# Five of the seven additions of squares in three norms, sent as accumulating transfers on GpSimd's queue

## Chip, cores and metric

One NeuronCore of a Trainium2 chip runs the whole program. The metric is the device time of one execution in microseconds; before, the median of 3 runs is 1616.66 us (1616.23 to 1616.78).

## The reference, cut to what matters

A trunk of two layers is applied to two groups of tokens, 512 and 256, which the kernel handles as 768 columns (`T`). The model has 1024 features, eight blocks of 128 rows.

```python
def rms_norm(x, g):
    y = xf * lax.rsqrt(jnp.mean(xf * xf, axis=-1, keepdims=True) + EPS)
    return y * g
...
for i in range(DEPTH):
    h = rms_norm(x, norm_mix[i])
    x = x + (window_attention(h, ...) if i % 2 == 0 else short_conv(h, ...))
    h = rms_norm(x, norm_mlp[i])
    x = x + jnp.square(jax.nn.relu(h @ mlp_w_up[i])) @ mlp_w_down[i]
    gate = jax.nn.sigmoid(rms_norm(x, norm_ple[i]) @ ple_w_gate[i])
    x = x + (p[i] @ ple_w_proj[i]) * gate
return rms_norm(x, final_norm)
```

## The kernel before, in words

**Precision and products.** Every factor is split into a high and a low half (`hi` by ScalarE, `lo` as a subtraction on VectorE), and each product takes three matmuls. Wide products use a scheme with seven instead of eight block products (`Norm7`, `Weights7`, `seven_parts`, line 2013), for which weights and activations are also summed and split (`q`, `t`, `sum`, `zhi`, `whi`, `vhi` and their low halves). The order inside one `seven_parts` is: product w11 into bank a, copy c of a (line 2030), product s3 into b, copy p, product s2 into a, copy d of a (line 2042), and so on. TensorE can't write on in bank a before ScalarE has made c, and again d.

**A norm.** The input of a norm comes in eight blocks, in the order 0, 4, 1, 5, 2, 6, 3, 7 (`PAIRED`, line 1911). For each block `Norm7.block` (line 729) splits the scaled block and calls `square` (line 620): the first block's square is written to `acc` by ScalarE (line 623); each later one goes to a temporary `sq` on ScalarE (line 626) and is added to `acc` by VectorE (line 627), seven additions of 128x768. When all are in, `acc` is split into `ah` and `al` (line 498 and 499), TensorE sums over the partitions by a matmul with ones (`ss`, line 666), and logarithm, exponential and one Newton step give the factor that later results are multiplied by. The products behind the norm start before the factor is known.

**The three norms of the change** are n1 (before the first MLP, its blocks come from the attention's output product), n3 (before the convolution, blocks from the gated layer `ple`) and n4 (before the second MLP, blocks from the convolution's output product). I call them norm 1, 3 and 4. Norm 2 and 5 (class `Norm`) keep their additions on VectorE.

**GpSimd's queue.** It issues accumulating transfers for two other purposes: `gathered` (line 830 to 837) sums pieces of the first weights behind norm 1 and norm 3 (four each), and `shared` (line 2224 to 2232) adds `p` to two halves of `x` in the MLPs (96 in all, 192 KB each). Its memory for descriptors is 512 bytes per partition (line 54).

**Buffers.** `sq`, `q`, `ah`, `al` and other temporaries share a ring of six buffers (`big`, line 580): a buffer can be written again when its last reader is done.

**The order of the work.** Behind the attention stage every operation is recorded, with a cost and a lag from `Recorder.add` (line 233), and `Recorder.end` (line 284) fixes the order of every engine from these estimates; then everything is issued in that order. A transfer on GpSimd's queue is entered with cost 3.5 and lag 5.0. Each engine runs its list in order, and waits on semaphores where a datum comes from another engine or from a transfer. GpSimd waits likewise: a transfer into `acc` is issued when the one before has landed.

Of the kernel before, what the change touches and what calls it, by code (L numbers as in the profile page):

```python
# [14 lines left out]
F32 = mybir.dt.float32  # L15
# [3 lines left out]
ALU = mybir.AluOpType  # L19
# [4 lines left out]
P = 128  # L24
# [3 lines left out]
T = sum(SEQS)  # L28
# [22 lines left out]
ROWS = 32  # L51
EXP_LN = "natural_log_exp_and_others"

BACC = dict(dynamic_dma_scratch_size=512)


class Tile:
# [89 lines left out]
class Recorder:  # L147
# [85 lines left out]
    def add(self, engine, what, run, outs, ins, line, table=None):  # L233
        n = max([1] + [size(ap) for ap in outs])
        if engine == "PE":
            cost = {384: 0.1735, 256: 0.121, 512: 0.23, 128: 0.11}.get(n, n * 0.45e-3)
            lag = cost + 0.16
        elif engine == "DVE":
            cost = 0.07 + n * 1.042e-3 + 0.06 * (what == "scalar_tensor_tensor" and n > 384)
            lag = cost + 0.082  # L240
        elif engine == "ACT" and what == "dma_start":
            cost, lag = 0.1, 4.0
        elif engine == "ACT":
            cost = 0.032 + n * 0.911e-3 + 0.09 * (len(ins) > 1)
            lag = cost + 0.095
            if table is not None:
                if table != self.tables[0]:
                    cost += 1.3
                    lag += 1.3
        elif engine == "SP":  # L250
            cost, lag = 0.46, 4 * P * n / 350e3
        elif what == "dma_start":
            cost, lag = 3.5, 5.0
        else:
            cost, lag = 0.3, 0.4
        op = Recorded(engine, run, cost, lag, line)
        op.size, op.due = n, self.due
        for ap in ins:
            self.touch(op, ap, False)
        for ap in outs:  # L260
            self.touch(op, ap, True)
        if self.also is not None:
            op.pre[self.also] = True
        if table is not None:
            if self.tables[1] is not None:
                op.pre.setdefault(self.tables[1], False)
            self.tables = table, op
        self.ops.append(op)
        return op
# [187 lines left out]
def trunk_kernel(ctx: ExitStack, tc: tile.TileContext, a: dict, out: bass.AP):  # L457
    nc = tc.nc
# [6 lines left out]
    const = ctx.enter_context(tc.tile_pool(name="const", bufs=1))  # L465
# [16 lines left out]
    sink = const.tile([P, HEADS], F32, name="sink")  # L482
    nsink = const.tile([P, HEADS], F32, name="nsink")
    ident = const.tile([P, P], F32, name="ident")
    make_identity(nc, ident[:])
    sparks = const.tile([P, P], BF16, name="sparks")
    dve.memset(sparks[:], 1.0)
    ones32 = const.tile([P, P], F32, name="ones32")
    dve.memset(ones32[:], 1.0)
    ones = const.tile([P, P], F32R, name="ones")  # L490
    dve.tensor_copy(ones[:], ones32[:])
    eps = const.tile([P, 1], F32, name="eps")
    dve.memset(eps[:], EPS)

# [104 lines left out]
    class Norm:  # L599


        n = T

        def __init__(self, i, name, places, acc, rstd=None):
            self.i, self.name, self.places, self.rplace = i, name, places, rstd
# [14 lines left out]
        def square(self, m, xb):  # L620
            if not self.begun:
                self.begun, self.acc = True, slot(self.aplace, f"acc_{self.name}", F32)[:, : self.n]
                act.activation(self.acc, xb, AF.Square)
            else:
                sq = self.temp("sq")
                act.activation(sq, xb, AF.Square)
                dve.tensor_tensor(self.acc, self.acc, sq, ALU.add)

        def temp(self, name, dt=F32):
            if more is not None:  # L630
# [16 lines left out]
                    act.preload_act_table_set(EXP_LN)  # L647
            self.ready = True

        def sum_squares(self, psum, also=None, parts=None, tag=None):  # L650

            n = self.n
            ah, al = parts or self.acc_parts()
            terms = [(ones, ah), (ones, al)]
            if also is not None:
                sq = self.temp("sq")
                dve.tensor_tensor(sq, also, also, ALU.mult)
                terms.append((ones32, sq))
            if more is None:
                t = psum.tile([P, 1024], F32, tag="mm", name="ss")  # L660
                out = [(t[:, :512], 0, 512), (t[:, 512:n], 512, n)]
            else:
                out = pieces(both("ss", tag)) if n == T else [(fresh("ss")[:, :n], 0, n)]
            for t, o, e in out:
                for i, (w, z) in enumerate(terms):
                    pe.matmul(t, lhsT=w[:], rhs=z[:, o:e], start=i == 0, stop=i == len(terms) - 1)
            return out
# [2034 lines left out]
    def conv_sources(n):  # L2702

        m = 2 * (n // 3) + (KB, 2 * KB, 0)[n % 3]
        return a["w_in"][m], a["w_in"][m + 1]
# [136 lines left out]
    held0 = [xs0[i] for i in (1, 2, 4, 5, 7, 8, 10, 11, 26, 27)] + act0[:2] + xs0[12:16] + act0[2:3]  # L2842

    n1 = Norm7(2, "mlp0", xs0[:12], act0[11], apart=xs0[12:], aside=act0[1])
    behind, product, w0 = second_inputs(n1, act0[7:11])
    w = [weight(a["w_o0"][2], 4)] * 2
    w2 = weight(a["w_o2"], 2, tag="z")
# [24 lines left out]
    act1 = ls[:7] + hs[4:8] + free[24:26] + ls[7:]  # L2872

    n3 = Norm7(1, "mix1", xs2, act0[9], aside=xs0[10])
    w2, behind = first_chunk(conv_sources(0), n3, 2, True)
    ple(n2, n3, act0[10:13], behind, w)

    n4 = Norm7(3, "mlp1", xs1, act1[11])
    w1, behind = first_chunk((a["up"][1, 0], a["up"][1, 2]), n4, 3, False)
    mixer_conv(n3, *w2, 2, n4, wide, xs0[16], ys, hs, ls, behind, (act0[13], xs0[11]))  # L2880
    spare = [xs1[i] for i in (21, 10, 11, 17, 0, 7, 14, 12, 13, 18, 19, 20, 24, 25)]
# [89 lines left out]
```

## Time and profile before

| | |
|---|---|
| median of 3 runs | 1616.66 us |
| the profiled execution: its time, its span | 1616.74 us, 1614.9 us |
| granted clock of TensorE | 0.998 |
| busy TensorE, VectorE, ScalarE, GpSimd | 1604.0, 1385.1, 958.9, 107.0 us |
| blocks of norm 1, norm 3, norm 4 | about 259 to 282, 774 to 828, 1010 to 1067 us |
| one addition of squares on VectorE | 0.945 us |

In rows of a timeline the columns are: start and duration in us, engine, line of the kernel, operation, written tile and read tiles, shape, count, and in brackets the idle time before and what ended it. In a list of waits they are: total us, times, longest. The busy time of TensorE contains the overlap of matmuls that follow each other, so a lost tenth of a microsecond shows rather in the distance of their starts. "issue" as a releaser means that the profile shows nothing that was waited for.

### The profile page before, as it was taken

To read this page: it belongs to the slowest core of one execution; us is meant where nothing else is said; L and a number is where in the kernel's file an instruction comes from. 1 tells how busy PE (TensorE), PEld (TensorE's weight loads), DVE (VectorE), ACT (ScalarE), POOL (GpSimd) and SP (SyncE) were. 2 spreads that over 40 slices of the span, in tenths; PEclk is the share of its full clock that TensorE was granted. 3 is DMA by queue.
4 is the path that set the end of the run, shared out by engine and by line. 5 is a ranking of instruction groups with operands and counts; after the bars stand their busy time and mean duration, and the time that the engine had idled before them with its cause. 6 is when DMAs were issued, how large, how long until landed. Compare 5 with 4: busy or idle time off the path is not lost.

```text
span 1614.9 us, 24411 instructions
## 1 busy us (share of the span) xinstructions
PE 1604.0 (99%) x9259; PEld 1556.6 (96%) x9259; DVE 1385.1 (86%) x2255; ACT 958.9 (59%) x1529; POOL 107.0 (7%) x166
## 2 busy tenths in 40 slices
PE   9999999999999999999999999999999999999997
PEld 7988889999999999999999999999999999999987
DVE  7579997998888888999899777789888888889985
ACT  7378887765555555556674434565555555556655
POOL 1001000010110110100000000000110111010000
PEclk9999999999999999999999999999999999999999
DMA  8745314233443343315312211112343343342232
GB/s 299 212 122 151 110 37 131 105 112 85 117 108 92 100 104 93 106 66 154 105 61 93 73 69 68 66 66 88 97 104 92 103 117 85 86 118 79 87 119 88
DMA packets 63953, 168.42 MB, mean 104 GB/s; under 512 B 7867, under 2 KB 23611, under 8 KB 63836
## 3 DMA queue, kind: packets, MB, share of 16 engines
q1 hardware_dynamic: 48716, 145.24, 26.8%
q0 software_dynamic: 14976, 21.50, 8.1%
q8 instruction: 72, 1.18, 0.3%
q14 instruction: 45, 0.37, 0.1%
q10 hardware_dynamic: 144, 0.13, 0.0%
HBM read 128.05 MB, written 9.96 MB: 85 GB/s over the span
## 4 chain that ended last, share of the span: by engine, by line
PE 95%; ACT 2%; DVE 2%; issue 1%; DMA 0%; SPq 0%; DVEq 0%; ACTq 0%
PE a L943 39%; PE b L943 10%; PE mm L435 8%; PE d L943 6%; PE c L943 5%; PE mm L557 5%; PE gate L557 4%; PE B L943 4%; PE C L943 4%; PE gate L2399 3%; PE O L435 2%; PE S L435 2%; PE pt L435 2%; PE vp L435 1%; DMA p<-in_p 0%
## 5 line engine op out<-in xcount | busy, mean ns | idle before, releaser
L922 DVE TENSOR_TENSOR zlo<-sum,zhi 128x1024 fp32r<-128x1024 f32 x76 | 92.8, 1221 | 66.9 <-ACT zhi L911 66.7
L2232 POOL DMA_DIRECT2D x<-p x96 | 83.9, 874 | 922.6 <-issue 704.0
L911 ACT ACTIVATE whi<-sum 128x1024 fp32r<-128x1024 f32 x76 | 80.7, 1062 | 99.3 <-PE a L943 88.6
L911 ACT ACTIVATE vhi<-wraw 128x512 fp32r<-128x512 f32 x76 | 48.0, 632 | 147.9 <-PE B L943 63.4
L943 PE MATMUL a<-xs,whi 128*128 128x384 f32 x696 | 135.5, 334 | 0.0
L943 PE MATMUL a<-t,zhi 128*128 128x384 f32 x604 | 124.3, 335 | 0.7 <-ACT c L2030 0.5
L943 PE MATMUL b<-t,zhi 128*128 128x384 f32 x604 | 123.5, 334 | 0.0
L943 PE MATMUL a<-t,whi 128*128 128x384 f32 x604 | 122.7, 335 | 0.3 <-ACT d L2042 0.3
L943 PEld LDWEIGHTS a<-xs,whi 128*128 128x128 f32 x696 | 121.9, 188 | 0.1
L943 PE MATMUL a<-act,whi 128*128 128x384 f32 x512 | 109.3, 334 | 0.0
L943 PEld LDWEIGHTS a<-t,zhi 128*128 128x128 f32 x604 | 106.2, 188 | 1.9 <-ACT c L2030 1.3
L943 PEld LDWEIGHTS a<-t,whi 128*128 128x128 f32 x604 | 106.1, 188 | 1.0 <-ACT d L2042 0.8
L943 PEld LDWEIGHTS b<-t,zhi 128*128 128x128 f32 x604 | 106.3, 188 | 0.5 <-DVE t L792 0.3
L911 ACT ACTIVATE zhi<-sum 128x1024 fp32r<-128x1024 f32 x76 | 80.6, 1061 | 43.9 <-PE a L943 33.8
L911 ACT ACTIVATE whi<-wraw 128x1024 fp32r<-128x1024 f32 x76 | 80.2, 1055 | 25.3 <-PE C L943 17.3
L922 DVE TENSOR_TENSOR wlo<-sum,whi 128x1024 fp32r<-128x1024 f32 x76 | 92.5, 1217 | 0.2 <-ACT whi L911 0.2
L922 DVE TENSOR_TENSOR wlo<-wraw,whi 128x1024 fp32r<-128x1024 f32 x76 | 92.6, 1218 | 0.0
L943 PEld LDWEIGHTS a<-act,whi 128*128 128x128 f32 x512 | 90.6, 188 | 0.0
L435 PE MATMUL mm<-xs_mix,whi 128*128 128x512 f32 (+1 forms) x320 | 80.1, 340 | 0.0
L2193 DVE TENSOR_TENSOR x<-x,a 128x384 f32<-128x384 f32 x128 | 67.5, 547 | 10.8 <-PE a L943 10.8
L786 ACT ACTIVATE t<-y 128x768 fp32r<-128x768 f32 x64 | 53.7, 839 | 36.6 <-DVE y L782 22.7
L943 PE MATMUL a<-xs,wlo 128*128 128x384 f32 x348 | 74.5, 334 | 0.0
(375 smaller groups left out, 4280.9 us busy)
## 6 DMA issues: line engine op xcount, KB each, us to landing
wraw<-in_up SPq DMA_DIRECT2D x64, 512.0 KB, 3.5
wraw<-in_down SPq DMA_DIRECT2D x64, 512.0 KB, 3.4
x<-p POOLq DMA_DIRECT2D x96, 192.0 KB, 3.2
wraw<-in_w_in SPq DMA_DIRECT2D x24, 512.0 KB, 3.4
wraw<-in_gate SPq DMA_DIRECT2D x16, 512.0 KB, 3.5
wraw<-in_w_q SPq DMA_DIRECT2D x8, 512.0 KB, 4.6
wraw<-in_w_out SPq DMA_DIRECT2D x8, 512.0 KB, 3.4
x_in<-in_x SPq DMA_DIRECT2D x8, 384.0 KB, 7.4
```

The source lines that it names most:

```text
L435: return f(*args, **kw)
L557: pe.matmul(t, lhsT=w, rhs=x[:, o:e], start=first and i == 0 and j == 0, stop=last and i == n - 1 and j == 2)
L786: act.activation(t[0][:], (self.q1, self.q2)[i][:], AF.Copy)
L911: act.activation(hi[:], src, AF.Copy)
L922: dve.tensor_tensor(lo[:], src, hi[:].bitcast(F32), ALU.subtract)
L943: pe.matmul(ps, lhsT=a, rhs=b, start=start and i == 0, stop=i == len(terms) - 1, skip_group_check=True)
L2193: dve.tensor_tensor(t[:, o : o + H], t[:, o : o + H], f, op)
L2232: pool.dma_start(low[i][:, o : o + H], p[:, i * H : i * H + H], accum_op=ALU.add)
L2399: pe.matmul(ps.t[:, o : o + n], lhsT=a_, rhs=b_, start=begin and i == 0 and j == 0, stop=end and i == len(terms) - 1 and j == 2,)
```

## The change

In the three norms, the additions of blocks 4, 1, 5, 2 and 6 become accumulating transfers from `sq` to `acc`, issued on GpSimd's queue; those of blocks 3 and 7, the last two, stay on VectorE. The memory for descriptors is doubled to 1024 bytes per partition; a tile of 512 bytes per partition (`ones32`) goes away, `ident` lends its place for the cast to `ones` and becomes the identity afterwards. An unused argument of `sum_squares` goes away. The recorder's estimate for a transfer on GpSimd's queue becomes 1.3 and 3.6.

```diff
-BACC = dict(dynamic_dma_scratch_size=512)
+BACC = dict(dynamic_dma_scratch_size=1024)
...
         elif what == "dma_start":
-            cost, lag = 3.5, 5.0
+            cost, lag = 1.3, 3.6
...
-    make_identity(nc, ident[:])
     sparks = const.tile([P, P], BF16, name="sparks")
     dve.memset(sparks[:], 1.0)
-    ones32 = const.tile([P, P], F32, name="ones32")
-    dve.memset(ones32[:], 1.0)
+    dve.memset(ident[:], 1.0)
     ones = const.tile([P, P], F32R, name="ones")
-    dve.tensor_copy(ones[:], ones32[:])
+    dve.tensor_copy(ones[:], ident[:])
+    make_identity(nc, ident[:])
...
-        n = T
+        n, sent = T, ()
...
                 act.activation(sq, xb, AF.Square)
-                dve.tensor_tensor(self.acc, self.acc, sq, ALU.add)
+                if m in self.sent:
+                    pool.dma_start(self.acc, sq, accum_op=ALU.add)
+                else:
+                    dve.tensor_tensor(self.acc, self.acc, sq, ALU.add)
...
-        def sum_squares(self, psum, also=None, parts=None, tag=None):
+        def sum_squares(self, psum, parts=None, tag=None):
...
     n1 = Norm7(2, "mlp0", xs0[:12], act0[11], apart=xs0[12:], aside=act0[1])
+    n1.sent = 4, 1, 5, 2, 6
...
     n3 = Norm7(1, "mix1", xs2, act0[9], aside=xs0[10])
+    n3.sent = 4, 1, 5, 2, 6
...
     n4 = Norm7(3, "mlp1", xs1, act1[11])
+    n4.sent = 4, 1, 5, 2, 6
```

Line numbers behind the changed places differ by one or two in the new kernel. Three places of the new order follow. First GpSimd, from the gathered weights of norm 1 (`sum<-in_up`, `sum<-sum`) to the last `shared`, before:

```order
L836 DMA sum<-in_up 128x1024
L836 DMA sum<-in_up 128x512 x2
L836 DMA sum<-sum 128x512
L2232 DMA x<-p 128x384 x48
L836 DMA sum<-in_w_in 128x1024
L836 DMA sum<-in_w_in 128x512 x2
L836 DMA sum<-sum 128x512
L2718 MEMSET z 128x1 x6
L2232 DMA x<-p 128x384 x48
```

and now (`acc_mlp_3320` is norm 1's sum, `acc_mix_8523` norm 3's, `acc_mlp_10633` norm 4's):

```order
L834 DMA sum<-in_up 128x1024
L834 DMA sum<-in_up 128x512 x2
L627 DMA acc_mlp_3320<-sq 128x768
L834 DMA sum<-sum 128x512
L627 DMA acc_mlp_3320<-sq 128x768 x4
L2230 DMA x<-p 128x384 x48
L834 DMA sum<-in_w_in 128x1024
L834 DMA sum<-in_w_in 128x512 x2
L834 DMA sum<-sum 128x512
L627 DMA acc_mix_8523<-sq 128x768 x5
L2716 MEMSET z 128x1 x6
L627 DMA acc_mlp_10633<-sq 128x768 x5
```

The first square of norm 1 stands between the gathered transfers, the other four behind them. Of the two `sum<-in_up` of 128x512, the one that needn't wait for the long one is now issued first.

Second, TensorE behind norm 1, where the first product (a) meets the sum over the partitions (`ss`); before:

```order
L943 MATMUL a<-xs_3408,whi 128x384
L943 MATMUL a<-xs_3457,whi 128x384
L943 MATMUL b<-t_3563,zhi 128x384
L943 MATMUL a<-xs_3457,whi 128x384
L943 MATMUL a<-xs_3315,wlo 128x384
L943 MATMUL a<-xs_3408,wlo 128x384
L943 MATMUL a<-xs_3457,wlo 128x384
L943 MATMUL b<-t_3609,zhi 128x384
L666 MATMUL ss<-al,ones 128x384 x2
L943 MATMUL a<-t_3449,zhi 128x384
L943 MATMUL a<-t_3492,zhi 128x384
L943 MATMUL a<-t_3473,zhi 128x384
```

and now, from the first matmul of a on:

```order
L941 MATMUL a<-xs_3315,whi 128x384 x2
L941 MATMUL a<-xs_3410,whi 128x384 x2
L941 MATMUL a<-xs_3528,whi 128x384 x2
L941 MATMUL a<-xs_3315,wlo 128x384
L941 MATMUL a<-xs_3410,wlo 128x384
L941 MATMUL a<-xs_3528,wlo 128x384
L664 MATMUL ss<-ah,ones 128x384
L664 MATMUL ss<-al,ones 128x384
L664 MATMUL ss<-ah,ones 128x384
L664 MATMUL ss<-al,ones 128x384
L941 MATMUL b<-t_3384,zhi 128x384
L941 MATMUL b<-t_3423,zhi 128x384
```

Before, the two matmuls of `ah` stood behind the third of a, and those of `al` ten matmuls later; now nine matmuls of a come first, then all four of ss, then nine of b, nine of a, nine of c, and only then the matmul that needs d: 40 in all.

Third, ScalarE from `ah` of norm 1 to the copy d; before:

```order
L498 ACTIVATE ah<-acc_mlp_3320 128x768
L2002 ACTIVATE pjs<-pj 128x512
L647 ACT_TABLE_LOAD
L911 ACTIVATE whi<-sum 128x1024
L2002 ACTIVATE pjs<-pj 128x512
L2030 ACTIVATE c<-a 128x384
L911 ACTIVATE vhi<-wraw 128x512
L685 ACTIVATE ln<-ss,eps 128x384
L855 ACTIVATE closing<-wraw 128x256
L685 ACTIVATE ln<-ss,eps 128x384
L865 ACTIVATE closing<-wlo 128x256
L688 ACTIVATE y<-ln 128x768
```

(the next row is d, L2042) and now, from the second `pjs` on, with `ah`, the table load, `pjs`, `closing<-wraw` and `whi<-sum` ahead of it:

```order
L2000 ACTIVATE pjs<-pj 128x512
L736 ACTIVATE x_3643<-x,vec 128x384
L2028 ACTIVATE c<-a 128x384
L683 ACTIVATE ln<-ss,eps 128x384 x2
L741 ACTIVATE xs_3668<-x,vec 128x768
L858 ACTIVATE closing<-q 128x128
L686 ACTIVATE y<-ln 128x768
L736 ACTIVATE xs_3690<-x,vec 128x384
L2040 ACTIVATE d<-a 128x384
```

Three scalings of blocks (two of 128x384, one of 128x768), which ScalarE did ahead of `ah` before, now stand between `ah` and d; vhi and a copy for `closing` stand elsewhere. On VectorE, the two additions that are left in norm 1 stand directly ahead of the low halves of two xs blocks, zlo and al, with one instruction between them. In norm 4, the orders of TensorE and ScalarE behind the last block are the same as before.

More of the change, by code (lines that the diff above doesn't have):

```diff
@@ L654, in sum_squares @@
             terms = [(ones, ah), (ones, al)]
[L655 to L658, printed above, removed]
             if more is None:
```

## The prediction

> **What bounds the kernel now.** I read the page first, then who waited for whom on TensorE, then TensorE's timeline at its two ends.
>
> ```profile
> PE 1604.0 (99%) x9259; PEld 1556.6 (96%) x9259; DVE 1385.1 (86%) x2255; ACT 958.9 (59%) x1529; POOL 107.0 (7%) x166
> ```
> ```profile
> PE warm L435 <- DVE sparks L435: 1.1, 1, 1.1
> PE a L943 <- ACT c L2030: 0.5, 1, 0.5
> PE a L943 <- ACT d L2042: 0.3, 1, 0.3
> PE mm L435 <- ACT whi L435: 0.3, 1, 0.3
> PE O L435 <- DVE heads L435: 0.2, 1, 0.2
> PE a L943 <- ACT t L786: 0.2, 1, 0.2
> ```
> ```profile
> 1.06 4.02 PE L435 MATMUL warm<-sparks 128*128 128x512 bf16 x9 [1.06 <-DVE sparks L435]
> ...
> 1606.50 0.28 PE L2399 MATMUL gate<-whi,xs_ple 128*128 128x256 f32 x1
> ```
>
> TensorE is idle for 1614.9 - 1604.0 = 10.9 us. Of these 1.1 us lie before its first matmul and 1614.9 - 1606.8 = 8.1 us behind its last, where the change does nothing. So 1.7 us of idle time is all that the middle holds, and the waits that belong to the three changed norms are 0.5 + 0.3 (norm 1) and 0.2 us (norm 4). Busy time hides a little more, because matmuls overlap. I therefore count by starts: a run of 128x384 matmuls costs 4.16 / 24 = 0.173 us each.
>
> ```profile
> 463.09 4.16 PE a L943 x24
> ```
> ```profile
> 287.48 0.68 PE L943 MATMUL a<-xs,whi 128*128 128x384 f32 x3
> ...
> 290.57 0.52 PE L666 MATMUL ss<-al,ones 128*128 128x384 f32 x2
> 291.61 0.79 PE L943 MATMUL a<-t,zhi 128*128 128x384 f32 x3 [0.53 <-ACT c L2030]
> ...
> 293.82 0.69 PE L943 MATMUL c<-xs,whi 128*128 128x384 f32 x3
> 294.83 0.44 PE L943 MATMUL a<-t,whi 128*128 128x384 f32 x1 [0.32 <-ACT d L2042]
> ```
>
> Behind norm 1, TensorE starts 34 matmuls between 287.48 and 294.83 us: 7.35 us for 34 x 0.173 = 5.88, so 1.47 us are lost, nearly all at the two waits for ScalarE's copies c and d. The table by stretches shows why those copies are late: both helpers are full.
>
> ```profile
> 269.00:276.00 7.00, 7.00 (x43) 7.00 (x42) 7.00 (x13) 7.00 (x10) 0.89 (x1) 1.00 0.55 127
> ...
> 283.00:290.00 7.00, 7.00 (x35) 5.97 (x34) 7.00 (x10) 6.95 (x12) 0.00 (x0) 1.00 0.52 187
> 290.00:297.00 7.00, 6.16 (x34) 5.50 (x33) 7.00 (x10) 7.00 (x15) 0.00 (x0) 1.00 0.19 67
> ```
>
> (Columns: length, then busy time of PE, PEld, DVE, ACT, POOL, the granted clock, the DMA share, GB/s.) A saving of more than about 2 us is not to be had here, whatever DVE is spared.
>
> **The change, part by part.** *The five additions.* One takes 0.945 us of VectorE, so each norm is spared 4.7 us. That is worth something only where TensorE waits for it.
>
> ```profile
> L627 DVE TENSOR_TENSOR acc_mlp<-acc_mlp,sq x7: 943/945/951, 264.1 to 285.5; 128x768 f32<-128x768 f32 x7
> ```
> ```profile
> 828.00:838.00 10.00, 10.00 (x60) 9.92 (x59) 10.00 (x16) 9.78 (x14) 0.00 (x0) 1.00 0.15 52
> ```
> ```profile
> 1066.67 1.02 DVE L1908 TENSOR_TENSOR x<-x,mm 128x384 f32<-128x384 f32 x2 [3.70 <-PE mm L557]
> ```
> ```profile
> 756.37 16.64 PE gate L557 x96
> ```
>
> Norm 4: VectorE has been idle for 3.70 us before the last block, so there is no backlog to shorten; the additions behind the last block are the two that stay. Worth 0. Norm 3: VectorE is full, but no wait of TensorE there is in the list (its shortest entry is 0.2). Worth 0 to 0.6; I take 0.2. In both, a block lasts 16.64 / 2 = 8.3 us on TensorE, twice what a transfer will be found to take below, so the chain of transfers keeps up, and if it didn't, each microsecond late would count as below.
>
> Norm 1 decides. Its blocks come faster, and now the sum is a chain of five transfers in series (4, 1, 5, 2, 6), each waiting on GpSimd for the landing of the one before, and then two additions on VectorE. Call X the end of the last addition; before, it was 285.49 + 0.94 = 286.4. From X on ScalarE splits off ah, and behind ah on its in-order queue stand the table load, the copies, c and d.
>
> ```profile
> 284.15 0.94 DVE L627 TENSOR_TENSOR acc_mlp<-acc_mlp,sq 128x768 f32<-128x768 f32 x1
> 285.02 0.54 DVE L782 SCALAR_TENSOR_TENSOR q<-q 128x384 f32<-128x384 f32 x1
> 285.49 0.94 DVE L627 TENSOR_TENSOR acc_mlp<-acc_mlp,sq 128x768 f32<-128x768 f32 x1
> ```
> ```profile
> 262.80 0.83 ACT L626 ACTIVATE sq<-x 128x768 f32<-128x768 f32 x1
> ...
> 282.09 0.60 ACT L738 ACTIVATE x<-x,vec 128x384 fp32r<-128x384 f32 x1
> ...
> 283.33 0.92 ACT L743 ACTIVATE xs<-x,vec 128x768 fp32r<-128x768 f32 x1
> ...
> 287.00 0.84 ACT L498 ACTIVATE ah<-acc_mlp 128x768 fp32r<-128x768 f32 x1
> ...
> 291.49 0.61 ACT L911 ACTIVATE vhi<-wraw 128x512 fp32r<-128x512 f32 x1
> ...
> 293.24 0.42 ACT L865 ACTIVATE closing<-wlo 128x256 fp32r<-128x256 f32 x1
> ```
>
> Before, TensorE's matmul behind d resumed 294.83 - 287.00 = 7.83 us after ah began. In the new order of ScalarE three scalings (0.60, 0.92, 0.60) come in between ah and d, and vhi (0.61) and a closing copy (0.42) go out: 1.1 us more, so 8.9 after ah, or X + 9.0. With nothing to wait for, TensorE would be there after 40 matmuls of the new order, at 287.48 + 40 x 0.173 = 294.4. The loss is then X + 9.0 - 294.4, against 1.47 before: **norm 1 changes by X - 286.9**, and not by less than -1.5. Held back with the two additions, on VectorE, are the low halves of two xs blocks, zlo and al, which TensorE wants too; that path is a little shorter than ScalarE's. ScalarE's scaled copies q share six buffers with the squares, and some now wait for a landing; they come two blocks behind the square whose buffer they take, so I price that at 0, and at 1 us if the landings are late (it then adds to X).
>
> *The price of one transfer (393 KB within SBUF, summed) is in no row.* The nearest:
>
> ```profile
> L2232 POOL DMA_DIRECT2D x<-p x96: 859/872/887, 345.9 to 1439.8; - x96
> ...
> DMA to landing us min/median/max: 2.9/3.2/5.6
> ```
> ```profile
> sum<-sum POOLq DMA_DIRECT2D x2, 256.0 KB, 3.3
> ```
> ```profile
> 355.11 0.87 POOL L2232 DMA_DIRECT2D x<-p  x1 [5.03 <-ACT B L2188]
> 358.38 0.88 POOL L2232 DMA_DIRECT2D x<-p  x1 [2.39 <-issue]
> ```
>
> The undisturbed 192 KB transfer lands 2.9 us after its issue, the 256 KB one after 3.3: 0.4 us per 64 KB, so 2.9 + 3 x 0.4 = 4.1 for 384 KB. From the median (3.2 to 3.3) it would be 3.5. I take the middle, 3.8, for an undisturbed one. [...] From landing to the next issue 3.27 - 2.9 = 0.3 us go by. The first square is ready at 262.80 + 0.83, so the first issue is at about 263.9.
>
> Undisturbed: 263.9 + 5 x 3.8 + 4 x 0.3 = 284.1, then addition, one other instruction, addition, 2.28 us as in the rows above, and 0.1 to be told: X = 286.5, a change of -0.4. But the stage isn't undisturbed:
>
> ```profile
> 264.18 19.07 SPq L511 DMA_DIRECT2D wraw<-in_up  x3
> ```
>
> Three weight loads of 512 KB are issued from 264 us on, the queues are busy for half of 269 to 276, and the same GpSimd queue still carries the gathered weights. Such company costs x<-p 0.3 us in the median and 5.6 - 2.9 = 2.7 at worst. I add the median's 0.3 to each hop (4.1 in all): X = 288.0, **+1.1 us**. Bounds: 0 and two hops of 2.7, so -0.4 to +5.0.
>
> ```profile
> 266.32 0.87 POOL L836 DMA_DIRECT2D sum<-in_up  x1 [3.38 <-issue]
> ```
>
> *Descriptor memory.* 358.38 follows 355.11 by a landing, though the two write different columns (line 2231): one transfer at a time. Doubled, two can be in flight. For the 96 x<-p transfers that is worth 0, since nobody waited for them. In norm 1 it lets the second half of the gathered sums go before the first long one has landed and the first square follow at once; without it the chain would start at the earliest behind the third gathered transfer's slot, some 2.4 us later (266.32 instead of 263.9). The last gathered transfer, sum<-sum, now stands behind the first square's; its reader on ScalarE (whi) stands behind ah, at 287 or later, which covers that.
>
> ```profile
> 41.34 0.52 PE L435 MATMUL rt<-ident,rstd_mix 1*128 1x1 f32 x6
> ```
>
> *The rest.* The identity is now made behind the cast to ones; its first reader on TensorE is at 41.34 us, which hides a delay of a few microseconds.
> The unused argument of sum_squares, and the memory that ones32 gives to the descriptors, cost nothing. The new constants 1.3 and 3.6 only reorder; outside the first four tiles behind norm 1 and the first two behind norm 3, TensorE's order is the same.
>
> Sum: +1.1 (norm 1) - 0.2 (norm 3) + 0 (norm 4) = +0.9 us on the profiled execution's 1616.74 (span 1614.9 and 1.8 around it). The median of the runs is 0.1 lower, so 1617.6.
>
> **The rivals.** *Short hops.* If 384 KB cost hardly more than 256 KB (3.3 to 3.7 us each, company or not), X falls to 284.0 to 286.0, TensorE's two waits go, and with norm 3 the gain is 1.1 to 2.1 us: 1614.6 to 1615.6. [...] Against it: the step between minimum and 256 KB. *The chain becomes the bound (slower).* TensorE stands at ss until the fifth transfer has landed and two additions are done. Above a mean hop of 3.9 us (X = 286.9) it is a loss, and above 4.55 (X = 290.3, with norm 3's gain) one of over 3.2 us: 1619.9 to 1621.5, the last with two hops of 2.7 extra. For it: three loads in 20 us; against it: the three issues are spread over 19 us, and 276 to 283 may stay empty of loads. *The doubled memory doesn't take a second transfer beside the first*: the chain starts 2.4 us later, +3.3 in all, 1620.0. *GpSimd is kept from writing descriptors while VectorE works.* The 96 issues took 859 to 887 ns beside a VectorE that is 86% busy, so there is no sign of it; if each of the five issues had to wait out one VectorE instruction of 0.945, the chain would be 4.7 us later, near 1622. [...]
>
> **How the numbers follow.** Forecast (hop 3.9 to 4.55, -0.2 to +3.2): 0.45. Short hops, and undisturbed ones down to -0.6: 0.32. Chain as the bound: 0.17. Memory: 0.04. Lock: 0.02. A measurement of this kernel tells 0.2%, 3.2 us, from no change. Faster by that needs more than TensorE loses: 0.03. Slower: 0.17 + half of 0.04 + 0.02, 0.21. Same: 0.76. The range cuts the best tenth of the short hops and the worst tenth of the long chain: 1615.0 to 1620.6.
>
> **What would show it.** Right: five acc_mlp transfers 4.0 to 4.4 us apart on GpSimd's timeline of norm 1; X near 288; TensorE waiting at ss or at the copy c instead of at c and d, about 2.5 us in all; TensorE's small gaps behind norm 3 smaller by tenths, those behind norm 4 unchanged. Wrong: hops under 3.7 us, or over 4.6; a TensorE wait in norm 3 or 4 for a transfer; VectorE, spared 4.7 us, still ending al on time; or a stage outside the norms that moves by more than 0.5 us.

## The result, and the profile after

The changed kernel takes 1624.86 us in the median (5 runs, 1624.19 to 1625.86), the kernel before 1616.66 (5 runs, 1615.95 to 1617.22): ratio 1.0052, 95% interval 1.0040 to 1.0063. It is 8.2 us slower. The forecast was 1617.6 and its range ended at 1620.6, so the prediction was wrong. The profiled execution of the changed kernel has a span of 1624.1 us.

First the busy times, then TensorE's list of waits (total us, times, longest):

```profile
PE 1607.5 (99%) x9259; PEld 1559.6 (96%) x9259; DVE 1375.2 (85%) x2240; ACT 959.0 (59%) x1529; POOL 120.2 (7%) x181
```
```profile
PE a L941 <- DVE xs L737: 4.0, 1, 4.0
PE a L941 <- ACT c L2028: 1.2, 1, 1.2
PE warm L435 <- DVE sparks L435: 1.1, 1, 1.1
PE b L941 <- DVE t L790: 0.9, 1, 0.9
```

VectorE is spared 10 us and TensorE has gained three waits: 4.0 us behind norm 1, and 1.2 and 0.9 us behind norm 3. VectorE's share was never the point; these three waits are.

**Norm 1.** GpSimd's rows from the first square's transfer on (start, GpSimd's time for the issue, in brackets the idle time before and what ended it):

```profile
264.60 0.89 POOL L627 DMA_DIRECT2D acc_mlp<-sq  x1 [2.49 <-ACT sq L625]
265.62 0.88 POOL L834 DMA_DIRECT2D sum<-sum  x1
271.22 0.86 POOL L627 DMA_DIRECT2D acc_mlp<-sq  x1 [4.72 <-DMA acc_mlp<-sq]
275.95 0.86 POOL L627 DMA_DIRECT2D acc_mlp<-sq  x1 [3.87 <-ACT xs L741]
280.48 0.88 POOL L627 DMA_DIRECT2D acc_mlp<-sq  x1 [3.67 <-DMA acc_mlp<-sq]
285.26 0.87 POOL L627 DMA_DIRECT2D acc_mlp<-sq  x1 [3.90 <-DVE t L790]
```

The issues are 6.6, 4.7, 4.5 and 4.8 us apart. VectorE's first addition behind the chain starts at 289.59 us, 4.3 us after the last issue. The `ACT` and `DVE` names in brackets are those of engines that were done long before; the datum waited for is the landing (at 275.36 and 284.62 us, 0.6 ahead of the issue). Next, VectorE and TensorE:

```profile
284.31 0.95 DVE L790 TENSOR_TENSOR t<-q,t 128x768 fp32r<-128x768 f32 x1
289.59 0.96 DVE L629 TENSOR_TENSOR acc_mlp<-acc_mlp,sq 128x768 f32<-128x768 f32 x1 [4.33 <-DMA acc_mlp<-sq]
290.47 0.55 DVE L780 SCALAR_TENSOR_TENSOR q<-q 128x384 f32<-128x384 f32 x1
290.94 0.95 DVE L629 TENSOR_TENSOR acc_mlp<-acc_mlp,sq 128x768 f32<-128x768 f32 x1
291.80 1.15 DVE L737 SCALAR_TENSOR_TENSOR xs<-x,vec,xs 128x384 fp32r<-128x384 f32 x2
```
```profile
287.80 0.68 PE L941 MATMUL a<-xs,whi 128*128 128x384 f32 x3
292.47 1.22 PE L941 MATMUL a<-xs,whi 128*128 128x384 f32 x3 [3.99 <-DVE xs L737]
...
296.11 1.22 PE L941 MATMUL b<-t,zhi 128*128 128x384 f32 x6
```

VectorE stands 4.33 us in front of an addition that waits for a landing. Behind that addition in its in-order queue are the low halves of xs, and TensorE wants those after its third matmul of a. From 287.80 to 292.47 three matmuls start where 0.52 us would do: 4.15 us lost. From 292.47 to 296.11 another ten start (six of a, four of ss): 3.64 us for 1.73, so 1.91 more are lost, and the list shows no wait there. The table by stretches names the greater part (length, busy PE, PEld, DVE, ACT, POOL, then the granted clock of TensorE):

```profile
288.50:292.40 3.90, 0.00 (x0) 0.00 (x0) 2.81 (x5) 1.29 (x2) 0.00 (x0) 1.00 0.39 131
...
293.00:296.10 3.10, 3.06 (x10) 2.56 (x9) 3.10 (x4) 3.09 (x5) 0.00 (x0) 0.51 0.21 75
```

The granted clock was 0.50 from 292.65 to 296.06 us, for 3.41 us. The matmuls of a start 0.32 to 0.35 us apart in it, which makes some 1.5 of the 1.91 us; the other 0.4 are lost at ss, whose first matmul with al started at 295.01, when al was ready (294.95). So norm 1 loses 4.15 + 1.91 = 6.1 us against 1.47 before: +4.6.

**Norm 3.** GpSimd, ScalarE and TensorE of that place, each in its own fence:

```profile
806.86 0.86 POOL L627 DMA_DIRECT2D acc_mix<-sq  x1 [6.79 <-ACT gt L2318]
814.12 0.86 POOL L627 DMA_DIRECT2D acc_mix<-sq  x1 [6.40 <-ACT t L784]
819.93 0.86 POOL L627 DMA_DIRECT2D acc_mix<-sq  x1 [4.95 <-ACT closing L858]
```
```profile
825.53 0.94 ACT L753 ACTIVATE q<-x,vec 128x768 f32<-128x768 f32 x1 [2.04 <-DMA acc_mix<-sq]
```
```profile
830.38 1.03 PE L941 MATMUL b<-t,zhi 128*128 128x384 f32 x5
832.35 0.44 PE L941 MATMUL b<-t,zhi 128*128 128x384 f32 x1 [0.94 <-DVE t L790]
...
834.53 1.60 PE L941 MATMUL a<-t,zhi 128*128 128x384 f32 x6 [1.22 <-ACT c L2028]
...
839.33 1.20 PE L941 MATMUL a<-t,whi 128*128 128x384 f32 x6
```
```profile
835.30:838.70 3.40, 3.40 (x13) 3.40 (x12) 3.40 (x6) 1.60 (x4) 0.00 (x0) 0.51 0.00 0
```

ScalarE's scaled copy q starts at 825.53 us, when the last transfer (issued at 819.93) has landed: 5.5 us, with weight loads issued at 819.04 and 823.70. What stands behind q on ScalarE and VectorE runs late by that, up to `t` and the copy c. TensorE loses 1.10 us (5 matmuls in 1.97 us), then 1.49 (4 in 2.18), then 1.69 at half clock (18 matmuls from 834.53 to 839.33 in 4.80 us for 3.11): 4.3 together, where the list of waits before showed none.

**Norm 4** shows no new wait: its only entry there is `PE a L941 <- ACT t L784`, 0.2 us, as before.

Counted by starts, the two are 4.6 + 4.3 = 8.9 us. The two profiled executions differ by 1625.86 - 1616.74 = 9.1, the medians by 8.2.

### The profile page after: what moved, and what is told of

Read it like the earlier page. It is cut to its first block, busy times and chain, and to the rows that moved or that the text cites. A ratio compares the mean times of both kernels' runs of the same rounds, so it can differ in the third digit from the quotient of the medians.

```text
span 1624.1 us, 24461 instructions
## 1 busy us (share of the span) xinstructions
PE 1607.5 (99%) x9259; PEld 1559.6 (96%) x9259; DVE 1375.2 (85%) x2240; ACT 959.0 (59%) x1529; POOL 120.2 (7%) x181
## 4 chain that ended last, share of the span: by engine, by line
PE 77%; DVE 3%; DMA 1%; ACT 1%; issue 1%; DVEq 0%; ACTq 0%; POOLq 0%
PE a L941 39%; PE b L941 9%; PE d L941 6%; PE c L941 6%; PE B L941 4%; PE C L941 4%; PE mm L556 4%; PE gate L2397 3%; PE gate L556 2%; DMA acc_mix<-sq 1%; DMA wraw<-in_w_in 0%; DMA acc_mlp<-sq 0%; DVE x L2688 0%; PE a L953 0%; DVE x L2321 0%
## 5 line engine op out<-in xcount | busy, mean ns | idle before, releaser
L941 PE MATMUL a<-xs,whi 128*128 128x384 f32 x696 | 135.7, 335 | 4.0 <-DVE xs L737 4.0
L941 PEld LDWEIGHTS a<-xs,whi 128*128 128x128 f32 x696 | 122.1, 188 | 4.6 <-DVE xs L737 4.5
L941 PE MATMUL a<-t,zhi 128*128 128x384 f32 x604 | 123.7, 335 | 1.4 <-ACT c L2028 1.2
L941 PE MATMUL b<-t,zhi 128*128 128x384 f32 x604 | 123.0, 334 | 0.9 <-DVE t L790 0.9
L941 PE MATMUL a<-t,whi 128*128 128x384 f32 x604 | 122.3, 334 | 0.0
L941 PE MATMUL a<-act,whi 128*128 128x384 f32 x512 | 109.3, 334 | 0.0
L941 PEld LDWEIGHTS a<-t,zhi 128*128 128x128 f32 x604 | 106.3, 188 | 2.6 <-ACT c L2028 2.1
L941 PEld LDWEIGHTS b<-t,zhi 128*128 128x128 f32 x604 | 106.5, 188 | 1.3 <-DVE t L790 1.2
L941 PEld LDWEIGHTS a<-t,whi 128*128 128x128 f32 x604 | 106.1, 188 | 0.4 <-ACT d L2040 0.3
L941 PEld LDWEIGHTS a<-act,whi 128*128 128x128 f32 x512 | 90.6, 188 | 0.0
L784 ACT ACTIVATE t<-y 128x768 fp32r<-128x768 f32 x64 | 53.7, 839 | 43.5 <-DVE y L780 24.3
L941 PE MATMUL a<-xs,wlo 128*128 128x384 f32 x348 | 75.0, 336 | 0.0
```

The source lines that it names most:

```text
L784: act.activation(t[0][:], (self.q1, self.q2)[i][:], AF.Copy)
L941: pe.matmul(ps, lhsT=a, rhs=b, start=start and i == 0, stop=i == len(terms) - 1, skip_group_check=True)
```

## The experiments

Times in the table are medians of this kernel and of the kernel before on the same chip; the ratio has its 95% interval.

| run | this, before (us) | ratio |
|---|---|---|
| no square sent | 1616.62, 1616.31 | 1.0001 (0.9992 to 1.0010) |
| norm 1 alone | 1622.30, 1616.31 | 1.0037 (1.0024 to 1.0049) |
| norm 3 alone | 1619.52, 1616.31 | 1.0017 (1.0008 to 1.0025) |
| norm 4 alone | 1616.58, 1616.31 | 1.0000 (0.9991 to 1.0009) |
| lag 6.0 | 1617.87, 1616.55 | 1.0010 (1.0001 to 1.0020) |
| norm 3 alone, own buffer | 1616.94, 1616.55 | 1.0003 (0.9994 to 1.0012) |
| norm 1 alone, two sums (first try) | 1624.21, 1616.55 | 1.0048 (1.0035 to 1.0060) |
| norm 1 alone, blocks 4 and 1 | 1618.30, 1616.55 | 1.0012 (1.0003 to 1.0020) |
| norm 1 alone, two sums | 1615.69, 1616.22 | 0.9996 (0.9987 to 1.0005) |
| norm 1 alone, half width | 1620.26, 1616.22 | 1.0025 (1.0015 to 1.0034) |
| memory of 512 bytes | 1631.07, 1616.22 | 1.0091 (1.0077 to 1.0105) |
| lag 6.0, blocks 4 and 1 | 1616.07, 1616.22 | 0.9998 (0.9989 to 1.0007) |
| norm 3 alone, same order, block 6 apart | 1617.27, 1616.11 | 1.0005 (0.9997 to 1.0014) |
| norm 3 alone, same order, blocks 2 and 6 apart | 1616.88, 1616.11 | 1.0004 (0.9995 to 1.0013) |
| two sums and norm 4 | 1615.99, 1616.11 | 0.9998 (0.9990 to 1.0007) |

**Theory:** each loss belongs to the transfers of its norm. In norm 1 an in-order engine waits for the end of a slow chain, with work behind it that TensorE wants; in norm 3 a transfer holds a buffer that ScalarE wants. **Rivals:** the recorder's new constants or the memory reorder the work and lose it; the moment at which the sum is complete decides (my sum X - 286.9); the DMA engines lack room.

### Which part loses

Edit: of the three lines `n1.sent`, `n3.sent`, `n4.sent` none or one is left.

```diff
-    n1.sent = 4, 1, 5, 2, 6
...
-    n3.sent = 4, 1, 5, 2, 6
...
-    n4.sent = 4, 1, 5, 2, 6
```

No square sent:

> The changed kernel with no square sent: all 21 additions back on VectorE, but the doubled memory for descriptors, the moved identity and the recorder's constants 1.3 and 3.6 stay. Theory (each loss belongs to the transfers of its norm): 1616.5 to 1617.2, as before; at most the 0.3 us at the very start stay. Rival (the new constants or the memory reorder the work and lose it, without the transfers): 1619 or more, with TensorE's waits behind norm 1 or norm 3 still in the list.

Norm 1 alone:

> Squares sent in norm 1 only. Theory (the serial chain of five transfers ends 3.9 us later than forecast, and TensorE waits 4 us for low halves behind the late addition, then runs some 3 us at half clock): +4.4 to +5.0 us over before, 1621.0 to 1621.7. Rival (the norms work on each other: norm 1 loses because something upstream moved): a loss below 3 or above 6 us.

Norm 3 alone:

> Squares sent in norm 3 only. Theory (transfers of 5.5 to 7 us beside the weight loads hold the squares' buffers, ScalarE's scaled copies and all behind them run 2 us late, and TensorE falls to half clock for 3.3 us): +3.2 to +3.8 us over before, 1619.9 to 1620.5. Rival (norm 3 only loses as an aftermath of norm 1): 1616.5 to 1617.2.

Norm 4 alone:

> Squares sent in norm 4 only. Theory (no wait there, as in the trace of the changed kernel): 1616.5 to 1617.2. Rival (a small loss hidden in the sums): over 1618.

Without transfers nothing is lost: the constants 1.3 and 3.6, the doubled memory and the moved identity cost nothing by themselves that the interval (0.1%, 1.6 us) shows, nor does norm 4. Norm 3 alone loses 3.2 us, as expected; its executions spread from 1617.45 to 1620.76, and the profiled one, 1620.20, is among the long ones. Norm 1 alone loses 6.0, more than the 4.4 to 5.0 of the theory and just short of the rival's 6. The chain is paced as in the changed kernel (last issue at 284.75 us, VectorE waits 4.34 us), so there is no sign that something upstream moved. The list of waits and the clock show the difference:

```profile
PE a L941 <- DVE xs L737: 4.5, 1, 4.5
```
```profile
291.30:298.10 6.80, 6.14 (x18) 5.68 (x19) 6.80 (x10) 6.77 (x12) 0.00 (x0) 0.50 0.22 80
```

The wait is half a microsecond longer, but the half clock lasts 6.83 us instead of 3.41. In the traces of the kernel before and of the changed kernel the time between two changes of the clock is 1, 84, 158, 229 or 470 times 3.41 us, and 6.83 is twice that; my reading, from these few traces, is that the place of the wait in this grid counts. Here the clock fell at 291.34, 0.62 us before TensorE went on, and the 3.41 us that followed, 2.79 of them busy, didn't bring it back; in the changed kernel it fell at 292.65, 0.18 us after TensorE had gone on, and the next 3.41 us, 3.38 of them busy, did. The length of that stretch is not a steady price: between these two programs it makes (2.79 + 3.41 - 3.38) / 2 = 1.4 us, an estimate.

### Norm 1: the order behind the wait, or the moment of the sum

```diff
-            cost, lag = 1.3, 3.6
+            cost, lag = 1.3, 6.0
```

> The changed kernel with the recorder's lag for a transfer on GpSimd's queue set to 6.0 instead of 3.6 (about what a hop took: 4.1 to 7 us and 0.6 to the next issue); all 15 squares are sent. The recorder now puts the low halves of xs, zlo and others ahead of the two additions of norm 1 on VectorE. Theory (the additions were placed too early in in-order queues, for a landing that the recorder thought near; the work behind them is what TensorE waited for): TensorE's wait of 4 us behind norm 1 and the half clock after it go, norm 1 loses 0 to 1.5 us; with norm 3 between 0 and 3.5, 1616.5 to 1620. Rival (only the moment when the sum is complete counts, as in my sum X - 286.9; order doesn't help): norm 1 still loses 4 us or more, 1620.5 or more.

The loss falls from 8.2 to 1.3 us. VectorE's two additions now stand far behind the low halves, and on ScalarE the copies c and d (289.82 and 293.10 us) now stand ahead of ah (298.19). VectorE's rows, and TensorE's:

```profile
284.62 1.01 DVE L742 SCALAR_TENSOR_TENSOR xs<-x,vec,xs 128x768 fp32r<-128x768 f32 x1
...
295.73 0.95 DVE L629 TENSOR_TENSOR acc_mlp<-acc_mlp,sq 128x768 f32<-128x768 f32 x1
296.60 0.69 DVE L880 TENSOR_TENSOR sum<-wraw 128x512 f32<-128x512 f32 x1
297.20 0.95 DVE L629 TENSOR_TENSOR acc_mlp<-acc_mlp,sq 128x768 f32<-128x768 f32 x1
```
```profile
287.00 1.23 PE L941 MATMUL a<-xs,whi 128*128 128x384 f32 x6
...
299.18 0.59 PE L664 MATMUL ss<-ah,ones 128*128 128x384 f32 x2
...
305.46 1.16 PE L941 MATMUL a<-t,zhi 128*128 128x384 f32 x5 [1.33 <-ACT c L2028]
```

The sum is complete at 297.20 + 0.95 = 298.15 us, 6.3 later than in the changed kernel, and TensorE doesn't stand for it: `ss` moved to 299 us, between other products. By X - 286.9 this run would lose 11 us in norm 1; what is left there is the wait of 1.33 at 305 us. So the moment of the sum alone doesn't decide: it costs what stands behind it in the queues. The rival, my own formula, falls for this order; it was made for one with c and d behind ah. The run moved both queues at once, so it doesn't tell what the low halves and what c and d would cost alone. Norm 3 gains from the new order too: TensorE's wait for `t` there is 0.3 instead of 0.9, and that for c is gone.

### Norm 3: the buffer, or the order

First the squares of blocks 2 and 6 in a place outside the ring, which also gave ScalarE and VectorE another order:

```diff
+    n3.own, n3.apart_sq = act0[13], (2, 6)
...
-                sq = self.temp("sq")
+                sq = slot(self.own, "sq", F32)[:, : self.n] if m in self.apart_sq else self.temp("sq")
```

> Squares sent in norm 3 only, and those of blocks 2 and 6 written to a buffer of their own outside the ring of six. Theory (a square's buffer is held until its transfer lands, and ScalarE's scaled copy that takes this buffer next waits for it): ScalarE's wait for a landing goes, TensorE's waits behind norm 3 go with it, 1616.3 to 1617.2. Rival (the sum itself is late, or the new order of the work loses): TensorE's waits stay, 1619.0 to 1620.

The loss is gone, but the order had changed as well. So two more runs keep every engine's order exactly as with norm 3 alone (the recorder is told of the old buffer, the square lies in another place):

```diff
+                ring = sq = self.temp("sq")
+                if m in self.apart_sq:
+                    sq = slot(self.own, "sq", F32)[:, : self.n]
+                    sq.tile.hidden = True
...
+    n3.own, n3.apart_sq = xs2[19], (6,)
```

Block 6 apart:

> Norm 3 alone, with every engine's order exactly that of the run with norm 3 alone; only the square of block 6, the last one sent, lies in a place of its own instead of a buffer of the ring. Theory (ScalarE's scaled copy waits for the landing of the fifth transfer because that holds the buffer): ScalarE's wait of 2 us for a landing goes, TensorE's waits of 1.0 and 1.2 us behind norm 3 and the half clock go, 1616.3 to 1617.2. Rival (the new order of the work behind norm 3 loses, and the buffer is only where it shows): 1619 to 1620, TensorE's waits unchanged.

Blocks 2 and 6 apart (`(2, 6)` in the last line):

> The same with the squares of blocks 2 and 6 in that place. Theory: as with block 6 alone, 1616.3 to 1617.2, since the fourth transfer has landed before its buffer is wanted. Rival (the fourth transfer's hold delays ScalarE too): at least 0.5 us less than with block 6 alone.

ScalarE's copy with norm 3 alone, and the same copy with block 6 apart:

```profile
819.92 0.94 ACT L753 ACTIVATE q<-x,vec 128x768 f32<-128x768 f32 x1 [2.13 <-DMA acc_mix<-sq]
```
```profile
818.68 0.92 ACT L762 ACTIVATE q<-x,vec 128x768 f32<-128x768 f32 x1
```

ScalarE doesn't wait, though the transfers were no faster (6.3 us in the median of the five, against 5.6), and TensorE's waits for `t` and for c behind norm 3 are gone. With nothing but the place of one square changed, the run falls from 1.0017 to 1.0005, with both squares 1.0004: no difference from the kernel before that the interval shows. The intervals of these runs and of norm 3 alone overlap, so it is the traces that decide: with the same order, ScalarE's wait for a landing, TensorE's two waits and the half clock (0.55 and 0.59 in the two stretches of 2 us from 829 us on) are there in one. TensorE's two waits are absent in the two others, and with block 6 apart ScalarE's is too, and its copy d starts 2.48 us behind c instead of 3.58. The buffer is the cause in norm 3, and the fifth transfer's is the one; blocks 2 and 6 apart took 0.4 us less than block 6 alone, too little to tell from noise.

### Norm 1: what the chain costs

Two sums by turns, so that two chains of two transfers fly at once. In the first try the second sum lay in a place that was read until 273 us:

```diff
+            elif self.second is not None and m == 4:
+                self.acc2 = slot(self.second, "acc2", F32)[:, : self.n]
+                act.activation(self.acc2, xb, AF.Square)
...
+                    if self.second is not None and m == 3:
+                        dve.tensor_tensor(self.acc, self.acc, self.acc2, ALU.add)
...
-    n1.sent = 4, 1, 5, 2, 6
+    n1.sent = 1, 5, 2, 6
+    n1.second = act0[5]
```

> Squares sent in norm 1 only, into two sums by turns: block 4 starts the second sum on ScalarE, 1 and 2 go to the first, 5 and 6 to the second, and VectorE adds the two (four transfers, two chains of two, three additions on VectorE). Theory (the serial chain, each transfer waiting for the landing of the one before, made the sum late): the last landing falls from 289.6 to about 283, TensorE's wait is below 1 us, 1616 to 1617.5. Rival (what the transfers lose is room on the DMA engines beside the weight loads): two in flight take 6 to 8 us each, the last lands no earlier than 287, 1619 or more.

```profile
273.23 0.85 ACT L625 ACTIVATE acc<-x 128x768 f32<-128x768 f32 x1 [9.44 <-PE mm L556]
```

ScalarE waits 9.44 us for TensorE to be done with that place; the run says nothing on chains. With `n1.second = xs0[11]`:

> The two sums of norm 1 once more, the second sum now in the place that block 7's low half takes later (in the first try its place was read until 273 us, and ScalarE stood 9.4 us in front of it, so that run said nothing on chains). Theory (serial chain): last landing at 284 or earlier, TensorE's wait behind norm 1 below 1.5 us, 1616 to 1618. Rival (room on the DMA engines): transfers in flight together take 6 us or more, last landing 287 or later, 1619 or more.

GpSimd and VectorE:

```profile
268.61 0.88 POOL L631 DMA_DIRECT2D acc_mlp<-sq  x1 [3.81 <-ACT xs L742]
270.42 0.86 POOL L631 DMA_DIRECT2D acc<-sq  x1 [0.93 <-ACT sq L628]
275.51 0.86 POOL L631 DMA_DIRECT2D acc_mlp<-sq  x1 [4.23 <-DMA acc_mlp<-sq]
277.83 0.88 POOL L631 DMA_DIRECT2D acc<-sq  x1 [1.45 <-ACT sq L628]
```
```profile
280.90 0.96 DVE L633 TENSOR_TENSOR acc_mlp<-acc_mlp,sq 128x768 f32<-128x768 f32 x1
...
283.98 0.96 DVE L633 TENSOR_TENSOR acc_mlp<-acc_mlp,sq 128x768 f32<-128x768 f32 x1
```

The last issue is at 277.83 instead of 285.26 us, VectorE waits for no landing, and the loss is gone. One transfer fewer doesn't explain it: four in series from 268.61 us, 4.7 us apart as in the changed kernel, would land at about 286.9 (an estimate), and here VectorE has added both sums by 283.20. The serial chain was the cause of the late landing. That the loss went is not due to the chain alone, since the low halves of two xs blocks (278.98) also stand ahead of the additions now. The first two transfers took 6.3 and 6.4 us, beside a weight load, `sum<-sum` and each other; the last two, in flight together for 1.6 us, took 3.9 and 4.0. And X, now 284.94, is 1.5 us earlier than before, which bought nothing on TensorE:

```profile
PE a L947 <- ACT c L2034: 0.6, 1, 0.6
...
PE a L947 <- ACT d L2046: 0.2, 1, 0.2
```

It waits for c and d nearly as long as before (0.5 and 0.3). ScalarE was busy without a gap up to ah, which began at 286.25, only 0.75 us earlier than before, and in the new order more stands between ah and d. The gain that the forecast gave to an early sum was not to be had.

Only blocks 4 and 1 sent (`n1.sent = 4, 1`), with lag 3.6:

> Only the squares of blocks 4 and 1 sent, in norm 1 only. Theory (a chain that ends before VectorE wants the sum costs nothing, and spares VectorE two additions where it is full): landing of the second at about 275.5, last addition at 284.5 to 286.4, TensorE's two waits of 0.8 us shorter or gone, 1615.2 to 1616.6. Rival (any transfer into the sum between the gathered weights makes VectorE's queue wait): 1618 or more, with VectorE waiting for a landing.

It missed: +1.75 us. VectorE waited only 0.42 us for a landing, so the rival's reason is not right either; the recorder put four of the five additions that are left close together (282.00 to 286.96 us) ahead of the low halves, and TensorE waits 1.2 us for these. With lag 6.0, norm 4's five transfers and none in norm 3:

> A candidate: lag 6.0 in the recorder, in norm 1 only blocks 4 and 1 sent, in norm 3 none, in norm 4 five. Theory (late landings are planned for, the chain of two ends before its sum is wanted, and VectorE is spared two additions): 1615.5 to 1616.8, same as before or a little under. Rival (VectorE's spared time in norm 1 is worth nothing, and the first transfer beside the gathered sum costs something in any order): 1617.5 or more.

It is the same as before within the interval, though TensorE still waits 1.7 us for a low half of xs in the profiled execution (at 1617.62 the slowest of eleven). Half of each square by transfer, the other half on VectorE:

```diff
-                    pool.dma_start(self.acc, sq, accum_op=ALU.add)
+                    pool.dma_start(self.acc[:, :H], sq[:, :H], accum_op=ALU.add)
+                    dve.tensor_tensor(self.acc[:, H:], self.acc[:, H:], sq[:, H:], ALU.add)
```

> Squares sent in norm 1 only, and of each only the first 384 of the 768 columns: 192 KB a transfer; VectorE adds the other half. Theory (a hop is mostly fixed: what the forecast took from 2.9 us for 192 KB and 3.3 for 256): hops of 2.9 to 3.3 us instead of 3.9 to 4.1, landing to next issue 0.6 as before, so the pitch falls from 4.6 to about 3.7, the chain ends 3.5 to 5 us earlier, loss 0 to 2.5 us: 1616.5 to 1619. Rival (each hop waits for engines or for the square, not for its own bytes): pitch stays above 4.4, 1620 or more.

```profile
264.86 0.89 POOL L627 DMA_DIRECT2D acc_mlp<-sq  x1 [4.58 <-ACT sq L625]
...
272.19 0.86 POOL L627 DMA_DIRECT2D acc_mlp<-sq  x1 [5.53 <-DMA acc_mlp<-sq]
275.76 0.86 POOL L627 DMA_DIRECT2D acc_mlp<-sq  x1 [2.71 <-ACT t L785]
```
```profile
271.70 0.94 ACT L754 ACTIVATE q<-x,vec 128x768 f32<-128x768 f32 x1 [3.40 <-DMA acc_mlp<-sq]
```
```profile
PE pj L1989 <- DVE wlo L498: 2.9, 1, 2.9
PE a L942 <- DVE xs L738: 1.1, 1, 1.1
```

The later issues are 3.6 us apart, with a median landing of 3.0: the 192 KB price was right, and half the bytes cost three quarters of a hop. The loss (4.0 us) was not 0 to 2.5: the first hop, beside a weight load and `sum<-sum`, takes 6.7 us at half the bytes too (7.3 to the next issue, less 0.6), and holds a buffer that ScalarE's copy wants, which waits 3.40 us. VectorE, which works on that copy, stands 3.17 us, and its low half `wlo` comes late for TensorE by 2.9. It is the mechanism of norm 3 in norm 1. The other 1.1 us are the late end of the chain again: VectorE still stands 2.01 us for the last landing, with low halves behind it.

### The doubled memory

```diff
-BACC = dict(dynamic_dma_scratch_size=1024)
+BACC = dict(dynamic_dma_scratch_size=512)
```

> The changed kernel with the memory for descriptors back at 512 bytes, all 15 squares sent. Theory (doubled, it lets the gathered sum and the first square of norm 1 be in flight together, which lengthens both; single, they follow each other): transfers one at a time; the first square's landing between 269 and 273, so norm 1 loses the same within 2.5 us, 1623 to 1627.5. Rival (the two in flight together are what made the first hop 6 us, so that one at a time ends the chain sooner): 1622.5 or less.

```profile
269.93 0.89 POOL L627 DMA_DIRECT2D acc_mlp<-sq  x1 [5.27 <-issue]
```
```profile
273.98 0.94 ACT L753 ACTIVATE q<-x,vec 128x768 f32<-128x768 f32 x1 [5.04 <-DMA acc_mlp<-sq]
```
```profile
PE a L941 <- DVE xs L737: 8.1, 1, 8.1
```

Another 6.2 us slower than the changed kernel, and beyond both expectations. One transfer at a time, the first square's issue is at 269.93 instead of 264.60 us, ScalarE's copies stand behind it, and TensorE's wait doubles; the half clock lasts 10.24 us, the greater part of it within that wait. The first hop took at most 4.05 us here (to 273.98), with `sum<-sum` only behind it (issued at 274.18). The memory is worth 6 us to this change (and nothing without it, as the run with no square sent shows).

### The candidate

Two sums in norm 1, five transfers in norm 4:

```diff
+    n1.second = xs0[11]
...
     n4.sent = 4, 1, 5, 2, 6
```

> The best version so far and norm 4: two sums in norm 1 (four transfers), five transfers in norm 4, none in norm 3. Theory (norm 4 neither gains nor loses): 1615.2 to 1616.2. Rival (VectorE's spared time in norm 4 shortens the small waits there): below 1615.2.

1615.99 us, no faster than with two sums in norm 1 alone. The best that the runs found, 0.9996 (0.9987 to 1.0005), is faster than the changed kernel by some 9 us, but not shown to be faster than the kernel before.

## Why the prediction was wrong

By the profiled execution, norm 1 cost 4.6 us where 1.1 were forecast, and norm 3 cost 4.3 where a gain of 0.2 was.

- **The hop, and so X: mis-sized.** The forecast's last landing was 288.0 less two additions and what lies between (2.38), 285.6 us; VectorE went on at 289.59. The first issue was 0.7 us later. The five hops, measured from issue to landing, took 6.0, 4.1, 3.9, 4.1 and 4.3 us instead of five times 4.1: the price was right for the last four, the first was 1.9 too long. A weight load was issued 0.07 us before that one and `sum<-sum` 1.0 us behind it. Norm 4's transfers, alone on their queue, took 7.0, 5.5 and 6.0 us with a weight load issued within 0.4 us, and 4.2 and 4.4 with none so near (1.14 and 0.95 us before), so the load is the likelier cause; no run moves one. From landing to the next issue 0.6 us pass, not 0.3: I had taken the median spacing of one pair less the shortest landing of 96. 0.7 + 2.0 + 1.3 are the 4.0 missing. The bounds, -0.4 to +5.0, did hold norm 1, but two long hops at 2.7 were named as the end of the range and not of the likely.
- **"That path is a little shorter than ScalarE's": this step failed.** TensorE waited for the low halves behind the two additions on VectorE, not for c and d: 4.15 us there and 1.91 behind it, in place of 1.47. ScalarE's path came out as long, though. ScalarE worked without a gap from ah (291.92 us) until d was done (300.90), and TensorE's matmul behind d started at 300.96, which is X + 9.07 where the sum had X + 9.0. That is why X - 286.9, +5.0 for the measured X of 291.89, came near the +4.6 of the trace. With the low halves on time TensorE would have stood at c and d to the same moment; that is worked out from these rows, and no run shows it. With norm 1 alone (X 291.37, so +4.5) the low halves and the longer half clock took more, +6.0. With c and d ahead of ah the formula is wrong by 10 us (lag 6.0).
- **The ring of six, put at 0 or at 1 us and only in norm 1: this step failed.** "The chain keeps up" in norm 3 was right: the last issues there are 7.3 and 5.8 us apart, they keep up with the blocks of 8.3 us, and the sum was not late. But I asked only when the sum is complete. The price of the buffer that is held until a landing was a wait of 2.04 us for a landing on ScalarE and 4.3 us on TensorE.
- **The half clock was in no term.** It is some 1.5 us of norm 1's loss and 1.7 of norm 3's, over a third of the whole. The granted clock was 0.50 for 3.41 us in each, and for 6.83 and 10.24 us, two and three times that, with norm 1 alone and with 512 bytes. Of the 3.41 us ahead of the fall TensorE was busy for 0.18 in norm 1, but for 1.80 in norm 3, where its two idle times were 0.94 and 1.22 us: no single long wait was needed there.
- **Right:** norm 4 (0), the constants and the identity (0), the x<-p transfers (0, though their median landing rose from 3.2 to 5.1 us, with up to three in flight and not two), the second transfer beside the first, and 4.1 us for 384 KB in four hops of five. The memory was worth 6.2 us and not 2.4.
- **The rivals.** The one with the chain as the bound (1619.9 to 1621.5) came nearest for norm 1, which alone took 1622.30, but it had TensorE standing at `ss`. TensorE stood before that, at a matmul whose operand was queued behind the same wait. GpSimd was not held up by VectorE in its issues (0.02, "Lock"): the 15 squares' took 0.86 to 0.89 us each, as forecast.

Two things stay open: how busy TensorE must be in a stretch of 3.41 us to keep its clock (1.80 us lost it in norm 3, and 2.24 kept it near the end of the changed kernel), and whether the weight loads are what lengthens a hop, since no run moves them.

## What to carry to other kernels

When an addition is moved from an engine to an accumulating transfer, count four prices: the landing (here 3.9 to 4.4 us for 384 KB, and 5.5 to 7.0 where a weight load was issued within 0.9 us), the gap to the next issue (0.6 us), the buffer that is held until the landing (2.04 us of waiting on ScalarE in norm 3), and everything queued behind the instruction that waits for the end of the chain (4.0 us of waiting on TensorE in norm 1). A planner that orders in-order queues must know the real lag: with 3.6 the changed kernel lost 8.2 us, with 6.0 it lost 1.3. And a wait on TensorE is to be priced with the half clock that may follow it, not only by its length: here 3.41 us of it followed the waits of 0.9 and 1.2 us in norm 3, and none a wait of 2.9 us (half width).

## What the runs showed of the hardware

- In the traces of the kernel before and of the changed kernel TensorE's granted clock was 1.00 or 0.50, and the time between two changes was 1, 84, 158, 229 or 470 times 3.41 us. Of the stretches of 3.41 us between, it fell behind those in which TensorE was busy for 0.00 and 0.72 us (the ends of the two traces), 0.18 (norm 1 of the changed kernel) and 1.80 (norm 3); behind all others, with 2.24 us or more, a clock of 1.00 stayed.
- It was at 0.50 for 3.41 us behind a wait of 4.0 us and behind two of 0.9 and 1.2, for 6.83 us with one of 4.5 (norm 1 alone) and for 10.24 with one of 8.1 (memory of 512 bytes). Behind one of 1.2 us (blocks 4 and 1 alone) it stayed at 1.00, and behind one of 2.9 us (half width) matmuls of 128x512 start 0.23 us apart, as they do at 1.00 in the changed kernel.
- In the changed kernel's trace eight of the fifteen accumulating transfers of 384 KB within SBUF landed 3.9 to 4.4 us after their issue. The other seven took 5.5 to 7.0, each with a weight load of 512 KB issued at most 0.9 us before or after it, and none of the eight had a load so near. Transfers of 192 KB took 3.0 us in the median of five (half width). From the landing to the next issue that waits for it 0.6 us pass.
- With up to three in flight, 96 transfers of 192 KB took 5.1 us in the median (changed kernel) instead of 3.2 one at a time (kernel before). With 512 bytes of memory for descriptors there was never more than one in flight on GpSimd's queue, with 1024 up to three.
